# A hybrid decoder step: head 0's new memory as a unit of the projections, its q and k loaded beside the last unit, a reordered input stage, and the ones with the last score

## The chip, the core and the metric

The kernel runs on one NeuronCore of a Trainium2 chip. TensorE (PE) does the matrix products, VectorE (DVE), ScalarE (ACT) and GpSimd (POOL) the element-wise work, and SyncE (SP) issues the transfers between device memory and the core's own memory. Each of these engines takes its instructions in the order in which the program lists them and waits, where it must, for the others by semaphores. The metric is the device time of one execution in microseconds.

## The reference

One inference step of a decoder layer: 528 prompt tokens (16 learned ones and 512) and 8 x 4 sample tokens, 560 columns in all, pass one wide projection; a pooling branch and a matrix memory (mLSTM) of 4 heads with 512 x 512 memories run on it; both are projected, gated, added and normalised.

```python
hn = rmsnorm(x, norm_g)
proj = einsum('btd,dn->btn', hn, w_in)     # a, z, q, k, v, o, z_m, gates i/f, merge gates
# matrix memory, per head:
s   = einsum('bhtd,bhsd->bhts', q, k) * w_intra           # the scores, weighted by decays
num = einsum('bhts,bhsv->bhtv', s, v) + w_inter * einsum('bhtd,bhdv->bhtv', q, C)
kw  = k * w_state
C_new = decay * C + einsum('bhsd,bhsv->bhdv', kw, v)      # the new memory, an output
```

For the prompt the old memory is zero, so that a head's new memory is `kw^T v` over 528 tokens: four row blocks d of 128 rows, each a sum over four full token tiles of 128 and a small one of 16.

## The kernel before

Every product of fp32 numbers is made of three products of split halves (hi and lo): ScalarE rounds a hi copy, VectorE or GpSimd subtracts it for the lo rest. Tokens lie in five tiles (four of 128, a small tile 4 of 48).

**Input stage** (`begin`). The normalised input is transposed tile by tile on TensorE (`turn`); for each tile ScalarE copies hi halves (`hT_hi`) and the whole values (`X`), and VectorE makes `hT_lo`. `project(j, t0, t1, part)` issues products of the first two weight tiles j with columns t0 to t1: part 0 is hi and lo of the input with the weights' hi, part 1 the input's hi with the weights' lo. In parallel SyncE loads the gates' columns into `wg_raw`; they are split into `wg` and multiplied (L576). The sums of `X` (L546) and their halves `Sa`, `Sb`, `Sc`, `Sd` (L553, L551) serve the seven-product scheme of the later projections. `pA`, `pV` and `pT` are engines pinned in program order; what is not pinned is placed by a scheduler.

**Projections** (`projections`). A list of units; each unit has loads, weight splits (`ahead`), products, and evacuations. While unit t multiplies, the splits of unit t+1 and the loads of t+2 are issued, woven into its products. A unit of 256 weight columns (`quad`) has seven products p1 to p7 on TensorE. The last two units are called g6 and g7 here (L167); between them lie memory updates of the sample tokens (`C`, L1131 and L1140).

**Attention** (`attention`). Each head is a set of step lists: `keys` (load k rows, scale by decays: `kw`, L1341), `fetch` and `values` (load v, split into `vr`), `turns` (transpose `kw` on TensorE and split into `kwr`, with 16 rows kept in `st`/`kwst`), `rows` (`prompt_C`: for each d, 12 products `vr`,`kwr` and one `vpt`,`kwst`: the new memory, L1372 and L1373), `decays` (`load_rows` brings `bc`, 960 KB, by a broadcast from `rows_d`; POOL adds the mask, ScalarE takes the exponential, L1325), `parts` (load k and q, split into `khi`, `klo`, `qh`, `ql`), `scores` (L167 again: products of `qh`, `ql` with `khi`, `klo`, 12 for each token tile) and `numerators`. `weave` mixes lists evenly. In the kernel before, head 0's keys and its fetch of v run beside g7, its four turns lie inside and behind g7's products, and its `rows` stand at the start of attention, woven with its decays and parts and with head 1's values and keys.

Rings: the tiles `r` (`RS` = 12 slots) hold loaded k, q, v and `kw`; the ring `hl` holds split weights.

Of the kernel before, what the change touches and what calls it, by code (L numbers as in the profile page):

```python
# [8 lines left out]
F32 = mybir.dt.float32  # L9
# [7 lines left out]
P = 128  # L17
# [83 lines left out]
class Trunk:  # L101
# [264 lines left out]
    def begin(self):  # L366
# [161 lines left out]
        self.split(wg[:, :, 0:64], wg[:, :, 64:128], raw, A, G)  # L528
# [162 lines left out]
    def projections(self, rest):  # L691
# [19 lines left out]
        for h in range(H):  # L711
            if h:
                values += range(len(units), len(units) + 4)
                units += self.unit_v(h)
            units += [self.unit_q(h, 0), self.unit_q(h, 1), self.unit_k(h, 0), self.unit_k(h, 1)]
            n = len(units)
            for j in range(2):
                units += [self.unit_o(h, j), self.unit_zm(h, j)]
            for name, g in fills[h]:
                fill(name, g)  # L720
            if h == 0:
                m = len(units)
            room[h] = n
        end = len(units)
# [12 lines left out]
        self.early = self.head(0)  # L737
# [6 lines left out]
        for t, u in enumerate(units):  # L744
# [13 lines left out]
            ahead = units[t + 1].ahead if t + 1 < end else self.early.keys + self.early.fetch  # L758
# [452 lines left out]
    def attention(self):  # L1211
# [41 lines left out]
    def head(self, h):  # L1253
        nc, O = self.nc, self.O
        V, A, G = nc.vector, nc.scalar, nc.gpsimd
        qT, kT, vr, vc, kwT, og, Pt, own = [], [], [], [], {}, [], [], {}
# [15 lines left out]
        def value(name):  # L1272
            return self.vp.tile([P, 2, HD], F32R, tag="value", name=self.name(name), bufs=17)
# [93 lines left out]
        def prompt_C(d):  # L1367
# [5 lines left out]
            nc.tensor.matmul(pc, kwst[:96], self.vpt[h % 2][:96], start=False, stop=True)  # L1373
# [6 lines left out]
        def score(i):  # L1380
            n, w, t0, o = TILEN[i], SEGW[i], TSTART[i], SEGO[i]
# [114 lines left out]
        u.fetch = each(fetch, 0, 1, 2, 3, 4)  # L1496
        u.turns, u.rows = each(k_rows, 0, 1, 2, 3), each(prompt_C, 0, 1, 2, 3)
# [158 lines left out]
```

## Time and profile before

| what | value |
|---|---|
| median of 3 runs | 1123.2 us (1121.22 to 1124.22) |
| profiled execution, its own time | 1124.12 us |
| its span in the profile | 1122.3 us |
| TensorE busy | 1064.3 us, 95% of the span |
| VectorE busy | 826.9 us, 74% |
| ScalarE busy | 542.1 us, 48% |
| GpSimd busy | 152.5 us, 14% |
| mean granted clock of TensorE | 0.976 of full speed |

The profiled execution lies 0.92 us above the median, and 1.8 us of it lie outside the span. Busy shares are means over all stages; where TensorE sits idle is told by the timeline of the single stages.

### The profile page before, as it was taken

How to read it: one execution, taken by the hardware profiler on the slowest of the kernel's cores; microseconds unless marked ns; L12 is line 12 of the kernel's file. 1: busy time of each engine (PE TensorE's matmuls, PEld its weight loads, DVE VectorE, ACT ScalarE, POOL GpSimd, SP SyncE). 2: the span in 40 equal slices, each digit the busy share in tenths (PEclk: the TensorE clock that was granted, in tenths of full speed). 3: DMA queues.
4: the chain of work that ended last, by engine and by line, in shares of the span. 5: the costliest groups of instructions: out<-in, count | busy, mean ns of one | idle time of the engine just before them, and what ended most of it. 6: DMA issues, size and time to landing. Idle time of an engine off the chain costs nothing.

```text
span 1122.3 us, 19632 instructions
## 1 busy us (share of the span) xinstructions
PE 1064.3 (95%) x7390; PEld 959.8 (86%) x7390; DVE 826.9 (74%) x1342; ACT 542.1 (48%) x1027; POOL 152.5 (14%) x309
## 2 busy tenths in 40 slices
PE   6799999999999999999998999987998789999997
PEld 5689999869999869999778999976887689999876
DVE  5678888787789687889787898855787978444353
ACT  5666545334454445554254554466576665122232
POOL 3100120001200002100001100012454423100000
PEclk9799999999999999999999999988999899999999
DMA  8354556789557688466688387887767889423132
GB/s 201 74 184 124 154 154 216 251 299 279 182 180 259 192 293 265 135 219 229 211 293 252 125 286 256 272 277 246 259 227 242 279 287 353 139 76 95 58 109 85
DMA packets 159615, 233.33 MB, mean 208 GB/s; under 512 B 17321, under 2 KB 82085, under 8 KB 159513
## 3 DMA queue, kind: packets, MB, share of 16 engines
q1 hardware_dynamic: 159521, 232.09, 64.7%
q8 instruction: 58, 0.95, 0.4%
q14 instruction: 36, 0.29, 0.1%
HBM read 160.65 MB, written 70.93 MB: 206 GB/s over the span
## 4 chain that ended last, share of the span: by engine, by line
PE 74%; DMA 12%; DVE 5%; ACT 4%; issue 2%; SPq 2%; POOL 1%; POOLq 0%; DVEq 0%; ACTq 0%
PE ps L167 57%; PE ps L984 7%; PE ps L1131 3%; DMA v_d<-v 2%; PE ps L1372 2%; PE ps L1140 1%; DMA v<-v_d 1%; DMA ra<-in_w_in_dram 1%; PE ps L987 1%; DMA kw<-k_d 1%; PE ps L80 1%; DMA wraw<-in_w_in_dram 1%; DMA x<-in_x_prompt_dram 1%; DMA k<-k_d 1%; PE ps L1415 1%
## 5 line engine op out<-in xcount | busy, mean ns | idle before, releaser
L167 PE MATMUL ps<-hT_hi,w 128*128 128x272 f32 (+1 forms) x752 | 158.7, 292 | 0.0
L167 PEld LDWEIGHTS ps<-hT_hi,w 128*128 128x128 f32 x752 | 123.7, 189 | 4.9 <-issue 3.1
L167 PE MATMUL ps<-hT_lo,w 128*128 128x272 f32 (+1 forms) x376 | 108.7, 289 | 0.0
L1145 DVE SCALAR_TENSOR_TENSOR C<-C,sw,ps 128x512 f32<-128x512 f32 x128 | 89.5, 742 | 10.3 <-PE ps L1140 9.9
L206 DVE TENSOR_TENSOR wb<-rb,wb 128x1024 fp32r<-128x1024 f32 x47 | 57.5, 1223 | 38.9 <-ACT wb L203 38.7
L167 PE MATMUL ps<-hT_hi,wb 128*128 128x272 f32 (+1 forms) x376 | 80.5, 293 | 3.2 <-DVE q L254 3.2
L167 PE MATMUL ps<-Sc_hi,wa 128*128 128x272 f32 (+1 forms) x376 | 79.5, 291 | 3.3 <-ACT u L239 3.2
L167 PE MATMUL ps<-Sb_hi,wb 128*128 128x272 f32 (+1 forms) x376 | 80.0, 292 | 2.0 <-ACT p L239 1.4
L167 PE MATMUL ps<-Sd_hi,w 128*128 128x272 f32 (+1 forms) x376 | 79.8, 292 | 0.0
L203 ACT CAST wa<-ra 128x1024 fp32r<-128x1024 f32 x47 | 49.3, 1050 | 62.3 <-DVE ra L216 52.8
L167 PE MATMUL ps<-Sa_hi,wa 128*128 128x272 f32 (+1 forms) x376 | 78.7, 289 | 0.0
L167 PEld LDWEIGHTS ps<-hT_lo,w 128*128 128x128 f32 x376 | 70.8, 188 | 0.0
L1054 POOL COPY qm<-qw 128x16 f32<-128x16 f32 x32 | 8.1, 286 | 428.4 <-DVE qw L1051 428.4
L167 PEld LDWEIGHTS ps<-hT_hi,wb 128*128 128x128 f32 x376 | 63.1, 191 | 3.6 <-DVE q L254 3.6
L167 PEld LDWEIGHTS ps<-Sc_hi,wa 128*128 128x128 f32 x376 | 62.2, 189 | 4.0 <-ACT u L239 4.0
L167 PEld LDWEIGHTS ps<-Sb_hi,wb 128*128 128x128 f32 x376 | 62.2, 189 | 2.6 <-ACT p L239 1.6
L203 ACT CAST w<-rb 128x1024 fp32r<-128x1024 f32 x47 | 49.4, 1050 | 30.5 <-PE ps L167 17.6
L167 PEld LDWEIGHTS ps<-Sd_hi,w 128*128 128x128 f32 x376 | 62.8, 191 | 0.0
L167 PEld LDWEIGHTS ps<-Sa_hi,wa 128*128 128x128 f32 x376 | 62.0, 188 | 0.0
L206 DVE TENSOR_TENSOR w<-rb,w 128x1024 fp32r<-128x1024 f32 x47 | 57.4, 1222 | 3.2 <-ACT w L203 3.1
L206 DVE TENSOR_TENSOR wa<-ra,wa 128x1024 fp32r<-128x1024 f32 x47 | 57.3, 1219 | 0.0
L203 ACT CAST wb<-rb 128x1024 fp32r<-128x1024 f32 x47 | 49.1, 1046 | 15.9 <-DVE rb L216 15.7
(371 smaller groups left out, 3083.9 us busy)
## 6 DMA issues: line engine op xcount, KB each, us to landing
C<-in_state_C_dram SPq DMA_DIRECT2D x64, 512.0 KB
out_dram<-C SPq DMA_DIRECT2D x64, 512.0 KB
ra<-in_w_in_dram SPq DMA_DIRECT2D x47, 512.0 KB
rb<-in_w_in_dram SPq DMA_DIRECT2D x47, 512.0 KB
wraw<-in_w_in_dram SPq DMA_DIRECT2D x18, 512.0 KB
v<-v_d SPq DMA_DIRECT2D x32, 256.5 KB
wraw<-in_w_branch_mlstm_dram SPq DMA_DIRECT2D x16, 512.0 KB
k_d<-k SPq DMA_DIRECT2D x16, 280.0 KB
```

The costliest lines, as they stand in the source:

```text
L80: return self.tc.keep_in_program_order(getattr(self.engine, op)(*a, **k))
L167: self.nc.tensor.matmul(out, s, m, start=(first and j == 0), stop=(j == len(seq) - 1), skip_group_check=not check)
L203: A.copy(w[name][0], w[s])
L206: V.tensor_tensor(w[name][1], w[s], w[name][0].bitcast(F32), ALU.subtract)
L984: nc.tensor.matmul(pv[i], s, m[:, k2], start=(k == 0 and j == 0), stop=(k == 7 and j == 2))
L987: nc.tensor.matmul(pv[4][:112], self.hS[:, k], m[:, k2], start=(k == 0 and j == 0), stop=(k == 7 and j == 1))
L1054: G.tensor_copy(self.qm[h % 2][:, d, 4 * g:4 * g + 4, 4 * g:4 * g + 4], self.bview(qw)[:, 4 * g:4 * g + 4])
L1131: nc.tensor.matmul(self.pqc[h][r:r + 8], self.qm[h % 2][:, d, b], Cs[bb // 2][:, bb % 2], start=(d == 0 and g == 0), stop=(d == 3 and g == 1),
L1140: nc.tensor.matmul(pu, self.kwst[h, d][r:r + 12, g], self.vst[h][r:r + 12, g], start=True, stop=True, tile_position=(r, 0))
L1145: V.scalar_tensor_tensor(C, C, self.bview(self.sw[h][:, 0])[:, 4 * g + bb, 3:4], pu, ALU.mult, ALU.add)
L1372: nc.tensor.matmul(pc, w[:, s, i], vr[i][:, m], start=(i == 0 and j == 0), stop=False)
L1415: nc.tensor.matmul(pb[:, o:o + mv.shape[-1] - m], s, mv[:, m:], start=(j == 0), stop=(j == last[True]))
```

## The change

Seven edits in four places.

1. Input stage: `parts(2, 3)` and `parts(4)` become `parts(2, 3, 4)`, so that the hi copies of tile 4 stand before the `X` copies of tiles 2 to 4. The last four `project` calls run part 0 of both weight tiles before part 1. The hi copy of `wg` is pinned on ScalarE, in program order behind the `X` copies.
2. A new unit is inserted before g7: it loads v of head 0 (`fetch`) and makes `kw` and `vr` while g6 multiplies, and its products are head 0's four turns and its new memory (`rows`). Its `vr`, `kwr` and `vpt` come from the ring `hl`, its `kwst` from the ring `r`.
3. Beside g7 now run eight loads of head 0's k and q (`ready`); the splits still wait for attention. Head 0's `klo` are all made on VectorE (two of them were POOL's).
4. The small load of constants into `bc` ("ones", `c_sel`) moves from `load_rows` to the last score; attention starts with head 0's decays, woven with its parts and head 1's keys and values.

```diff
         project(1, 0, 256, 1)
-        parts(2, 3)
-        parts(4)
+        parts(2, 3, 4)
         for j in range(2):
             project(j, 256, NT, 0)
+        for j in range(2):
             project(j, 256, NT, 1)
...
         wg = gp.tile([P, NK, P], F32R, name="wg")
-        self.split(wg[:, :, 0:64], wg[:, :, 64:128], raw, A, G)
+        pA.copy(wg[:, :, 0:64], raw)
+        G.tensor_tensor(wg[:, :, 64:128], raw, wg[:, :, 0:64].bitcast(F32), ALU.subtract)
...
+        self.early = e = self.head(0)
+        units.insert(len(units) - 1, Unit(e.fetch, e.keys + e.values, [lambda: [f() for f in e.turns], *e.rows]))
         end = len(units)
...
-        self.early = self.head(0)
...
-            ahead = units[t + 1].ahead if t + 1 < end else self.early.keys + self.early.fetch
+            ahead = units[t + 1].ahead if t + 1 < end else self.early.ready
...
-        u = heads[0]
-        for f in (*u.values[:4], *u.turns, u.values[4]):
-            f()
-        weave(heads[0].rows, heads[0].decays, heads[0].parts, heads[1].values + heads[1].keys)
+        weave(heads[0].decays, heads[0].parts + heads[1].keys + heads[1].values)
...
-            raw = value("vr")
+            raw = self.hl("vr", 2, HD) if early else value("vr")
...
         def part_k(d):
-            t = self.r("k32")
-            nc.sync.dma_start(t, self.k_d[:, 4 * h + d])
-            kT.append(self.parts(t, lambda s: key("k" + s), G if d % 2 else V))
+            if ("k", d) not in qk:
+                fetch_k(d)
+            t = qk.pop(("k", d))
+            kT.append(self.parts(t, lambda s: key("k" + s), G if d % 2 and not early else V))
...
         def score(i):
+            if i == 4:
+
+                nc.sync.dma_start(bc()[48:80, SEGO[4]:SEGO[4] + 48], self.I["c_sel"])
...
         def load_rows():
             nc.sync.dma_start(bc(), self.rows_d[h, :OWI].partition_broadcast(P))
 
-            nc.sync.dma_start(bc()[48:80, SEGO[4]:SEGO[4] + 48], self.I["c_sel"])
-
...
+        u.ready = [f for i in range(4) for f in (*each(fetch_k, i), *each(fetch_q, i))]
```

Where the scheduler puts the instructions shows in their order on the engines, at three places. Line numbers of the changed kernel differ by up to 24 from those of the kernel before.

ScalarE in the input stage, before: `ps_302` and `ps_307` are tile 4, the other `ps` tiles 2 and 3.

```order
L80 COPY X<-ps_249 128x4x128
L138 CAST wg<-wg_raw 128x8x64
L80 COPY X<-ps_254 128x4x128
L80 COPY X<-ps_267 128x4x128
L80 COPY X<-ps_272 128x4x128
L80 CAST hT_hi<-ps_302 128x4x24 x2
L80 CAST hT_hi<-ps_307 128x4x24 x2
L80 COPY X<-ps_302 128x4x24 x2
L80 COPY X<-ps_307 128x4x24 x2
L553 CAST Sa_hi<-X 128x560 x2
```

The same place in the changed kernel:

```order
L80 CAST hT_hi<-ps_302 128x4x24 x2
L80 CAST hT_hi<-ps_307 128x4x24 x2
L80 COPY X<-ps_249 128x4x128
L80 COPY X<-ps_254 128x4x128
L80 COPY X<-ps_267 128x4x128
L80 COPY X<-ps_272 128x4x128
L80 COPY X<-ps_302 128x4x24 x2
L80 COPY X<-ps_307 128x4x24 x2
L80 CAST wg<-wg_raw 128x8x64
L554 CAST Sa_hi<-X 128x560 x2
```

The hi copies of tile 4 moved ahead of all `X` copies, and the copy of `wg`, which stood before three of them, now stands behind all and ahead of `Sa_hi`.

TensorE at the end of the projections, before: the last products of g7 (`hT_hi,wb`), the last turns of head 0 and the first new memory products (L1372).

```order
L167 MATMUL ps_8603<-hT_hi,wb_8586 128x272
L167 MATMUL ps_8603<-hT_lo,wb_8585 128x272
L167 MATMUL ps_8603<-hT_hi,wb_8585 128x272
L1360 MATMUL ps_8854<-ident,st_2_747 96x128
L1359 MATMUL ps_8865<-ident,kw_8686 128x128 x4
L1360 MATMUL ps_8866<-ident,st_3_749 96x128
L1372 MATMUL ps_8897<-vr_8817,kwr_8836 128x512 x3
L1372 MATMUL ps_8897<-vr_8820,kwr_8836 128x512 x3
L1372 MATMUL ps_8897<-vr_8823,kwr_8836 128x512 x3
```

The changed kernel, first where the turns now stand: in front of `hT_hi,wb`, which are here the last products of g6.

```order
L1378 MATMUL ps_8643<-ident,kw_8503 128x128 x4
L1379 MATMUL ps_8644<-ident,st_0_743 96x128
L1378 MATMUL ps_8655<-ident,kw_8525 128x128 x4
L1379 MATMUL ps_8656<-ident,st_1_745 96x128
L1378 MATMUL ps_8667<-ident,kw_8550 128x128 x4
L1379 MATMUL ps_8668<-ident,st_2_747 96x128
L1378 MATMUL ps_8679<-ident,kw_8556 128x128 x4
L1379 MATMUL ps_8680<-ident,st_3_749 96x128
L167 MATMUL ps_8473<-hT_hi,wb_8448 128x272
L167 MATMUL ps_8473<-hT_lo,wb_8447 128x272
```

and the end of the new unit, where g7 (`w_1406`) begins:

```order
L1394 MATMUL ps_8795<-vr_8576,kwr_8686 128x512 x3
L1394 MATMUL ps_8795<-vr_8594,kwr_8686 128x512 x3
L1394 MATMUL ps_8795<-vr_8597,kwr_8686 128x512 x3
L1394 MATMUL ps_8795<-vr_8616,kwr_8686 128x512 x3
L1395 MATMUL ps_8795<-vpt_8635,kwp_8689 128x512
L167 MATMUL ps_8813<-hT_hi,w_1406_8704 128x272
L167 MATMUL ps_8813<-hT_lo,w_1406_8704 128x272
```

All four turns now lie in one piece ahead of g6's last product, and all four new memory blocks ahead of g7, so that scores follow g7 directly.

ScalarE at the start of attention, before (`bc_8894` is head 0's decay rows, L1325 the exponentials; `vr_8885` belongs to head 1):

```order
L138 CAST vr_8885<-v_1425_8883 128x512
L138 CAST khi_8890<-k_1427_8888 128x560
L1325 ACT_TABLE_LOAD
L1325 ACTIVATE bc_8894<-bc_8894,acol 128x512
L1325 ACTIVATE bc_8894<-bc_8894,acol 128x400
L1325 ACTIVATE bc_8894<-bc_8894,acol 128x272
L1325 ACTIVATE bc_8894<-bc_8894,acol 128x144
L1325 ACTIVATE bc_8894<-bc_8894,acol 48x48
```

and in the changed kernel:

```order
L138 CAST khi_8992<-k_1437_8883 128x560
L138 CAST qh_8996<-q_1438_8885 128x544
L138 CAST khi_9000<-k_1439_8900 128x560
L1332 ACT_TABLE_LOAD
L1332 ACTIVATE bc_8976<-bc_8976,acol 128x512
L138 CAST qh_9006<-q_1441_8924 128x544
L1332 ACTIVATE bc_8976<-bc_8976,acol 128x400
L1332 ACTIVATE bc_8976<-bc_8976,acol 128x272
L1332 ACTIVATE bc_8976<-bc_8976,acol 128x144
L1332 ACTIVATE bc_8976<-bc_8976,acol 48x48
```

Before, one `khi` stood ahead of the exponentials and the other key and query halves behind; now all but the last `qh` stand ahead, and this last one behind the table load and the first exponential.

## Rows read from the trace of the kernel before

**Rows 1.** Timeline of TensorE, input stage (start us, duration us, instruction, [idle before <-releaser]).

```profile
35.22 0.62 PE L80 MATMUL ps<-hT_hi,whi 128*128 128x304 f32 x1 [8.99 <-ACT hT_hi L80]
41.32 0.30 PE L80 MATMUL ps<-hT_hi,whi 128*128 128x304 f32 x1
44.79 0.37 PE L576 MATMUL ps<-hT_lo,wg 128*128 128x280 f32 x1
49.92 0.40 PE L984 MATMUL ps<-wlo,hT_hi 128*128 128x512 f32 x1
```

**Rows 2.** Timeline of ScalarE, input stage.

```profile
32.80 0.62 ACT L138 CAST wg<-wg_raw 128x512 fp32r<-128x512 f32 x1 [7.06 <-DMA wg_raw<-in_w_in_dram]
34.76 0.69 ACT L80 CAST hT_hi<-ps 128x96 fp32r<-128x96 f32 x4
37.21 1.31 ACT L553 CAST Sa_hi<-X 128x560 fp32r<-128x560 f32 x2 [0.85 <-DVE X L546]
```

**Rows 3.** Timeline of VectorE, input stage and first gates.

```profile
35.20 0.75 DVE L80 TENSOR_TENSOR hT_lo<-ps,hT_hi 128x96 fp32r<-128x96 f32 x4 [8.28 <-ACT hT_hi L80]
39.05 0.73 DVE L551 TENSOR_TENSOR Sa_lo<-X,Sa_hi 128x560 fp32r<-128x560 f32 x1
47.95 0.50 DVE L582 SCALAR_TENSOR_TENSOR ig<-ps,gbi,ig 4x280 f32<-4x280 f32 x1 [1.16 <-ACT zf L581]
```

**Rows 4.** Timeline of GpSimd, input stage.

```profile
33.50 1.26 POOL L141 TENSOR_TENSOR wg<-wg_raw,wg 128x512 fp32r<-128x512 f32 x1 [9.95 <-ACT wg L138]
```

**Rows 5.** Timeline of TensorE, its two waits between 76 and 100 us.

```profile
79.56 0.40 PE L167 MATMUL ps<-Sb_hi,wb 128*128 128x272 f32 x1 [1.41 <-ACT p L239]
92.12 0.39 PE L167 MATMUL ps<-Sb_hi,wb 128*128 128x272 f32 x1 [0.62 <-DVE wb L206]
```

**Rows 6.** By stretch: length; PE, PEld, DVE, ACT, POOL busy; granted clock; DMA share; GB/s.

```profile
72.00:80.00 8.00, 6.59 (x41) 5.79 (x40) 3.60 (x4) 7.97 (x19) 0.00 (x0) 1.00 0.54 152
100.00:690.00 590.00, 583.33 (x4237) 524.18 (x4236) 481.90 (x773) 282.15 (x501) 42.62 (x138) 0.99 0.70 223
743.00:775.00 32.00, 20.81 (x74) 15.06 (x74) 13.76 (x23) 21.74 (x47) 8.00 (x21) 0.78 0.85 289
749.00:762.00 13.00, 13.00 (x47) 10.46 (x48) 3.36 (x6) 8.00 (x18) 3.83 (x10) 0.80 0.73 269
770.00:785.00 15.00, 13.09 (x78) 11.36 (x78) 11.25 (x24) 9.30 (x25) 4.19 (x8) 0.73 0.83 284
```

**Rows 7.** Timeline of TensorE, end of projections and start of attention.

```profile
728.14 0.29 PE L167 MATMUL ps<-hT_hi,w 128*128 128x272 f32 x1
748.87 12.56 PE L1372 MATMUL ps<-vr,kwr 128*128 128x512 f32 x43 [3.44 <-DVE kwr L141]
769.72 0.76 PE L167 MATMUL ps<-qh,klo 128*128 128x512 f32 x1 [4.08 <-ACT qh L138]
```

**Rows 8.** SyncE's queue, issues of head 0's kw and bc loads.

```profile
734.64 2.00 SPq L1339 DMA_DIRECT2D kw<-k_d  x2
746.39 0.32 SPq L1488 DMA_DIRECT2D bc<-rows_d  x1
```

**Rows 9.** Timeline of VectorE, the third kw of head 0.

```profile
739.19 0.71 DVE L1341 SCALAR_TENSOR_TENSOR kw<-kw,wsb 128x528 f32<-128x528 f32 x1 [3.35 <-DMA kw<-k_d]
```

**Rows 10.** Timeline of ScalarE, first decays of head 0.

```profile
752.60 1.28 ACT L1325 ACT_TABLE_LOAD   x1 [1.51 <-DMA bc<-rows_d]
753.89 2.19 ACT L1325 ACTIVATE bc<-bc,acol 128x512 f32<-128x512 f32 x5
```

**Rows 11.** Groups of ScalarE by shape, 690 to 800 us (busy us, mean ns | idle before).

```profile
L138 ACT CAST khi<-k 128x560 fp32r<-128x560 f32 x7 | 4.6, 658 | 0.8 <-DMA k<-k_d 0.8
```

**Rows 12.** Groups of VectorE by shape, 743 to 800 us.

```profile
L141 DVE TENSOR_TENSOR ql<-q,qh 128x544 fp32r<-128x544 f32 x6 | 4.3, 720 | 1.7 <-ACT qh L138 1.7
```

**Rows 13.** Timeline of GpSimd, first and last step of head 0's D chain.

```profile
783.94 0.66 POOL L1426 COPY D<-bc 128x112 f32<-128x112 f32 x1 [0.61 <-DVE bc L1385]
793.88 0.28 POOL L1430 TENSOR_TENSOR D<-D,bc 48x48 f32<-48x48 f32 x1
```

More of the change, by code (lines that the diff above doesn't have):

```diff
@@ L1255, in head @@
         V, A, G = nc.vector, nc.scalar, nc.gpsimd
-        qT, kT, vr, vc, kwT, og, Pt, own = [], [], [], [], {}, [], [], {}
+        qT, kT, vr, vc, kwT, og, Pt, own = [], [], {}, [], {}, [], [], {}
+        early = h == 0
         def bc():
@@ L1287, in load_v @@
             t = v32.pop(i) if i in v32 else rows_in(i)
-            raw = value("vr")
+            raw = self.hl("vr", 2, HD) if early else value("vr")
             self.split(raw[:m, 0], raw[:m, 1], t[:m, :HD], A, V)
-            vr.append(raw)
+            vr[i] = raw
             if i == 4:
+                if early:
+                    own["vpt"] = self.hl("vpt", HD)
+                    for k in range(4):
+                        G.tensor_copy(own["vpt"][:, k * P:(k + 1) * P], self.zeros)
+                else:
+                    own["vpt"] = self.vpt[h % 2]
                 for j, p in enumerate((0, 1, 0)):
-                    nc.sync.dma_start(self.vpt[h % 2][32 * j:32 * j + 16].bitcast(F32), raw[:16, p].bitcast(F32))
+                    nc.sync.dma_start(own["vpt"][32 * j:32 * j + 16].bitcast(F32), raw[:16, p].bitcast(F32))
         def centre(i):
@@ L1325, in decays, with fetch_q, fetch_k @@
             A.activation(w, w, AF.Exp, bias=self.acol[:n, i, h:h + 1])
+        qk = {}
+        def fetch_q(d):
+            t = qk["q", d] = self.r("q32")[:, :NO]
+            nc.sync.dma_start(t, self.q_d[:, 4 * h + d])
+        def fetch_k(d):
+            t = qk["k", d] = self.r("k32")
+            nc.sync.dma_start(t, self.k_d[:, 4 * h + d])
         def load_q(d):
-            t = self.r("q32")[:, :NO]
-            nc.sync.dma_start(t, self.q_d[:, 4 * h + d])
+            if ("q", d) not in qk:
+                fetch_q(d)
+            t = qk.pop(("q", d))
             qh, ql = key("qh"), key("ql")
@@ L1360, in k_rows @@
             nc.tensor.transpose(ps2[:96, :P], self.st2[d].bitcast(F32), self.ident)
-            w = value("kwr").rearrange("p s (i d) -> p s i d", i=4)
+            w = (self.hl("kwr", 2, HD) if early else value("kwr")).rearrange("p s (i d) -> p s i d", i=4)
             self.split(w[:, 0], w[:, 1], ps.rearrange("p (i d) -> p i d", i=4), A, V)
-            kwst = self.hp.tile([P, P], F32R, tag="kwst", name=self.name("kwst"), bufs=3)
+            if early:
+                kwst = self.r("kwp", F32R)[:, :P]
+            else:
+                kwst = self.hp.tile([P, P], F32R, tag="kwst", name=self.name("kwst"), bufs=3)
             A.copy(kwst[:96], ps2[:96, :P])
@@ L1372, in prompt_C @@
                     nc.tensor.matmul(pc, w[:, s, i], vr[i][:, m], start=(i == 0 and j == 0), stop=False)
-            nc.tensor.matmul(pc, kwst[:96], self.vpt[h % 2][:96], start=False, stop=True)
+            nc.tensor.matmul(pc, kwst[:96], own["vpt"][:96], start=False, stop=True)
             c32 = self.r("c32")[:, :HD]
```

## The prediction, made before the changed kernel ran

> **What bounds the kernel now.** I began with the busy time by stretch [rows 6]. From 100 to 690 us TensorE is busy 583.3 of 590 us at a clock of 0.99: there every microsecond by which its work starts earlier is kept, and nothing else counts. So a gain can come only from stretches in which TensorE stands idle or runs at half clock, and the change touches two. The first is the input stage: TensorE waits 8.99 us for a hi copy, until 35.22 [rows 1], and its next matmuls take 0.62 us each, against 0.30 at 41.32 [rows 1]: that is the lower level of its clock, 1.2 GHz, against 2.4. The second is the passage to attention: between 743 and 775 us it is busy 20.81 of 32 us, idle 11.2 [rows 6], and the granted clock is 0.80 between 749 and 762 and 0.73 between 770 and 785 [rows 6]. In time this costs 13 x 0.20 + 15 x 0.27 = 6.7 us. Both places together hold some 27 us; the question is how much of them another engine takes back.
>
> **Input stage, step by step.** ScalarE shows why TensorE waits: the copy of `wg` stands among the `X` copies and waits 7.06 us for its load, until 32.80, and tile 4's hi copies (0.69 us) stand behind it at 34.76 [rows 2]. VectorE has been free since 35.20 - 8.28 = 26.9 us [rows 3]. With the hi copies first, they lie in front of the wait; tile 4 was transposed before TensorE's idle time began at 35.22 - 8.99 = 26.2 us [rows 1]. So `hT_lo` is there by 26.9 + 0.75 = 27.7 us [rows 3], TensorE waits about 1 us, and if its clock stays up, the 48 products take twice the 3.4 us that the second 24 took between 41.32 and 44.79 [rows 1]: done at about 34.5.
>
> The gates come next. They need `wg`, whose load does not move: it lands at 32.80, its copy takes 0.62, its lo half on POOL 1.26 us from 33.50 [rows 2, 4], so that the gates can start at about 35, against 44.79 [rows 1]: 9.8 us earlier on TensorE. This isn't the gain. `Sa_hi` stands behind `wg` on ScalarE and can't start before 33.4; its first half takes 0.65, so VectorE starts `Sa_lo` at 34.1 instead of 39.05 [rows 2, 3]. Its chain from there to the lo half of the next weights ran without a gap to 47.95 - 1.16 = 46.8 [rows 3], 7.7 us, so it now ends at 41.8. The first product with those weights, at 49.92 [rows 1], comes at 41.9: 8.0 us earlier. The gate arithmetic behind it on VectorE, at 47.95 after 1.16 us of waiting for ScalarE [rows 3], starts at 41.9: 6.1 earlier. This chain leads over ScalarE, which is busy 7.97 of 8 us between 72 and 80 us [rows 6], to the wait of 1.41 us at 79.56 [rows 5]. There TensorE, 8.0 ahead, meets a ScalarE that is 6.1 ahead, and gives the difference back. The wait of 0.62 at 92.12 [rows 5] is for work that is then ahead and mostly goes. The term is **-6.6 us**, with bounds of -5.0 (only `Sa_lo`'s shift, 39.05 - 34.1, passes on) and -8.0 (all of TensorE's). Which part of `project` comes first costs nothing: the same 48 products, all operands present. POOL's two `hS` casts change places with `wg`'s lo half; they are covered by TensorE's products up to 34.5.
>
> **Passage to attention.** The new unit moves work and adds none: four turns, 52 products. That the new memory left its place behind g7 takes away the wait of 3.44 us ahead of it [rows 7], and the rest of the 11.2 us idle is no longer where it was, so the sum is that idle time against the new waits, counted from the changed order.
>
> - Turns in one piece, ahead of g6's last product: they need `kw`, and the products after them `kwr`. VectorE's added work there, some 13 splits and scalings of about 0.7 us [rows 9, 12], lies beside g6 and a new unit of about 12 us. I take 0.4 us; bounds 0 and the 3.44 of [rows 7].
> - First score behind g7: ScalarE must evacuate g7, then make `khi` and `qh` (0.66 each [rows 11]), VectorE `klo` (0.72 [rows 12]). Before, this was hidden by the new memory's products. About 2.0 us, bounds 1.4 and 4.08, the longest such wait now [rows 7].
> - Within the first score each d needs `klo` and `ql`, 1.4 us of VectorE [rows 12], for 0.7 us of TensorE: three times 0.7, 2.1 us; this includes `klo` moved from POOL to VectorE. The last `qh` stands behind the first exponential, which waits for `bc`. Its load took 752.60 - 746.39 = 6.2 us [rows 8, 10]; issued as g7 ends, it would leave some 4 us more. `bc`'s issue stands right behind `qc`'s, which ends during g7's last products, so I take none of it, and keep 4.4 as the bound.
> - Head 1's turns and its first new memory block: 1.0 us for `kw` and `kwr`, bounds 0 and 3.4.
> - Its second block: `kwr` stands on ScalarE behind the conversion of head 0's D and behind head 1's five exponentials (2.19 us [rows 10]). D comes from POOL, whose chain took 783.94 to 794.16, 10.2 us [rows 13]. From the first score on: 0.7 + 10.2 + 0.7 + 2.2 + three conversions of 0.7 = 15.9; TensorE's scores and turns meanwhile, 13.09 x 0.73 = 9.6 us at full clock [rows 6] less 1.4 for those of the first score, and 12 of the 43 products that took 12.56 at 0.80, 2.8 us [rows 6, 7], make 11. That is 4.9 us at most; as the chain had 1.5 us of waits for ScalarE and VectorE, I take 3.2.
>
> New waits: 0.4 + 2.0 + 2.1 + 1.0 + 3.2 = 8.7 us for 11.2, **-2.5 us**. The half clock I leave as it is: the new memory of head 0 escapes it (2.6 us), but waits of 2 to 3 us have been followed by it in this trace (3.44, then 0.80 [rows 6, 7]), and head 1's memory now stands behind such a wait. Bounds: 0 if waits take everything, -6.7 more if no half clock is left. The moved load of ones (`c_sel`) only takes an issue out of SyncE's way; it is covered by the scores. The k and q loads beside g7 are under products, at a DMA share of 0.85 now [rows 6].
>
> On ScalarE the table load takes 1.28 us and the exponential starts 0.01 us behind it [rows 10]. The Trainium skill (ScalarE: Activation LUTs, What ACT_TABLE_LOAD costs) puts a drain of about 1.38 us to each load, 2.66 in all. By the row the last `qh` waits for 1.28 us, by that rule for 1.38 us more, if it can't hide in the wait for `bc` that stands before the load here (1.51 us [rows 10]); the sum would then be -7.7 instead of -9.1.
>
> **Sum.** -6.6 - 2.5 = -9.1: the profiled execution of 1124.1 us (its span 1122.3, 1.8 around it) becomes 1115.0. It lies 0.9 above the median of the runs, so the median is about 1114.
>
> **Rivals.**
> Only the start counts: the waits in front of the scores take all 11.2 us. For it speaks that TensorE has no other work there any more; against, that all k and q lie loaded. -6.6, 1116.6 as a median.
> Full gain: scores follow g7 at full clock. For it: every operand is loaded; against: VectorE needs twice TensorE's time per score. -8.0 at the start, -6 of the idle time, -5 of the half clock: 1104.
> The start is eaten: if gates or weights in the first 100 us hang on a load instead of VectorE's chain, all comes back by 100 us, as `wg`'s load does not move. Then -2.5, perhaps -3: 1120.5.
> Slower: all four turns stand ahead of everything, so one late `kw` holds up TensorE. The third and fourth are issued behind stores of g6's results on SyncE, now at 734.64 [rows 8], and the first of them was scaled at 739.19 [rows 9], 4.55 us later. The turns would now start at 728.1 [rows 7], the third at 729; with 0.9 for scaling, the issue must come by 723.6. If it stays at 734.6, TensorE waits 11.0 us, and 2.6 of half clock follow: -9.1 + 13.6 = +4.5, a median of 1127.7. It makes the kernel slower by over 3.4 us from an issue at about 733.5 on. Against it: in the changed order `kw` needs no result later than g6's.
>
> **Chances.** Forecast (1110.5 to 1116.5) 0.57, start only (to 1118.5) 0.17, full gain (1103 to 1110) 0.12, start eaten 0.08, slower 0.06. A difference of 0.3%, 3.4 us, is about what can be told from none: faster means below 1119.8, slower above 1126.6. Faster takes the first three and a fifth of the fourth: 0.87; same 0.07; slower 0.06. The range leaves out the ends: 1106.5 to 1119.
>
> **What would show it.** Right: TensorE's first 304-column product near 27 us at 0.30 us each, the gates at 35, the product of 49.92 at 42, a longer wait near 72 us; in the passage no wait over 4 us, several of 1 to 3 ahead of scores and of head 1's memory. Wrong: half clock from 27 to 40 again; a wait over 3 us inside the turns; g7 waiting for its weights; a first score later than 3 us behind g7.

## The result, and the profile after

| | before | after |
|---|---|---|
| median of the runs compared, us | 1123.71 (4 runs, 1121.22 to 1126.98) | 1113.36 (4 runs, 1112.18 to 1113.63) |
| profiled execution / its span, us | 1124.1 / 1122.3 | 1112.18 / 1110.4 |
| mean granted clock | 0.976 | 0.987 |

The ratio is 0.9907, with a 95% interval of 0.9889 to 0.9926: the change takes 8.3 to 12.5 us off, 10.4 by the medians. About 1114 was predicted.

Timeline of TensorE in the input stage, which answers to [rows 1], and its two waits after 70 us, which answer to [rows 5]:

```profile
27.93 0.37 PE L80 MATMUL ps<-hT_hi,whi 128*128 128x304 f32 x1
29.15 0.41 PE L80 MATMUL ps<-hT_lo,whi 128*128 128x304 f32 x1 [0.85 <-DVE hT_lo L80]
29.39 0.30 PE L80 MATMUL ps<-hT_hi,whi 128*128 128x304 f32 x1
...
35.96 0.37 PE L577 MATMUL ps<-hT_lo,wg 128*128 128x280 f32 x1
...
41.51 0.50 PE L986 MATMUL ps<-wlo,hT_hi 128*128 128x512 f32 x1 [0.25 <-DVE wlo L975]
...
72.73 0.39 PE L167 MATMUL ps<-Sb_hi,wb 128*128 128x272 f32 x1 [2.90 <-ACT p L239]
76.31 0.39 PE L167 MATMUL ps<-Sc_hi,wa 128*128 128x272 f32 x1 [0.32 <-ACT u L239]
```

The wait of 8.99 us is a wait of 0.85, and the products behind it take 0.30 us, the time of the upper clock level (granted clock 1.00 from 28 to 34 us), from the third on. What lies ahead of the edits came late in this execution: tile 4's first transpose stands at 25.95 us, in before at 24.10, so that against [rows 1] the gain of the first products looks 1.9 us too small. Where the lead is handed back shows too: the wait for ScalarE's `p` is 2.90 us where [rows 5] had 1.41. In after the clock stayed at 1.00 behind it, but in eight of the twelve profiles with the new start it fell to the lower level there for 3 to 7 us (e1: 0.57 from 72 to 76 us), a price that the prediction doesn't have.

ScalarE, GpSimd and VectorE in the same stage, which answer to [rows 2 to 4]:

```profile
31.37 0.62 ACT L80 CAST wg<-wg_raw 128x512 fp32r<-128x512 f32 x1 [1.41 <-DMA wg_raw<-in_w_in_dram]
31.89 1.22 ACT L554 CAST Sa_hi<-X 128x560 fp32r<-128x560 f32 x2
```

```profile
32.07 1.78 POOL L529 TENSOR_TENSOR wg<-wg_raw,wg 128x512 fp32r<-128x512 f32 x1 [2.11 <-ACT wg L80]
```

```profile
29.99 2.70 DVE L547 TENSOR_TENSOR X<-X 128x560 f32<-128x560 f32 x4 [0.56 <-ACT X L80]
32.60 1.84 DVE L552 TENSOR_TENSOR Sa_lo<-X,Sa_hi 128x560 fp32r<-128x560 f32 x1
...
40.23 1.23 DVE L975 TENSOR_TENSOR wlo<-wraw,whi 128x1024 fp32r<-128x1024 f32 x1
41.36 0.49 DVE L583 SCALAR_TENSOR_TENSOR ig<-ps,gbi,ig 4x280 f32<-4x280 f32 x1
```

All eight `X` copies now lie ahead of `wg`, so ScalarE's wait fell from 7.06 to 1.41 us and VectorE could sum `X` from 29.99 on. The load itself was there 1.4 us earlier, which isn't the edits' doing (see e2). `Sa_lo` takes 1.84 us, not 0.73, while GpSimd works on `wg`.

The passage by stretch, which answers to [rows 6] (length; PE, PEld, DVE, ACT, POOL busy; granted clock; DMA share; GB/s):

```profile
690.00:719.70 29.70, 29.70 (x237) 27.21 (x236) 26.09 (x48) 15.26 (x34) 2.13 (x4) 1.00 1.00 350
719.70:738.00 18.30, 18.12 (x103) 14.44 (x102) 12.45 (x17) 9.11 (x18) 0.00 (x0) 1.00 0.42 151
738.00:754.00 16.00, 13.79 (x89) 12.10 (x88) 6.22 (x10) 10.29 (x23) 4.69 (x10) 0.90 0.77 244
754.00:775.00 21.00, 14.58 (x86) 11.82 (x85) 15.41 (x30) 15.13 (x40) 14.77 (x27) 0.91 0.84 295
775.00:797.00 22.00, 21.85 (x130) 19.70 (x131) 16.24 (x37) 15.75 (x39) 3.44 (x3) 0.93 0.88 289
```

and, overlapping these, the 32 us that [rows 6] shows from 743 on, and 13 us from the first score on:

```profile
743.00:775.00 32.00, 23.36 (x134) 18.91 (x132) 21.19 (x38) 23.96 (x58) 19.46 (x36) 0.89 0.82 276
750.00:763.00 13.00, 10.56 (x37) 7.55 (x38) 10.63 (x23) 9.57 (x25) 7.65 (x13) 0.74 1.03 353
```

From the first turn (719.7) to 797 us TensorE is idle 0.18 + 2.21 + 6.42 + 0.15 = 9.0 us; [rows 6] had 11.2, and 8.7 was predicted. Over the 32 us from 743 the clock is 0.89 where it was 0.78; half clock is left behind the first score's wait (0.74 from 750 to 763) and behind the one at 775.15. This last stretch lies just outside of the 32 us; from 715 to 800 us the clock is 0.94, in before 0.90.

Timeline of TensorE there, which answers to [rows 7]:

```profile
721.70 0.66 PE L1378 MATMUL ps<-ident,kw 128*128 128x128 f32 x4 [0.18 <-ACT kwp L1386]
...
725.30 3.04 PE L1394 MATMUL ps<-vr,kwr 128*128 128x512 f32 x12
...
750.14 0.47 PE L167 MATMUL ps<-qh,klo 128*128 128x512 f32 x1 [2.05 <-DVE klo L141]
750.77 0.80 PE L167 MATMUL ps<-ql,khi 128*128 128x512 f32 x1 [0.17 <-DVE ql L141]
...
756.01 0.49 PE L167 MATMUL ps<-qh,klo 128*128 128x512 f32 x1 [1.48 <-ACT qh L138]
756.77 0.50 PE L167 MATMUL ps<-ql,khi 128*128 128x512 f32 x1 [0.27 <-DVE ql L141]
...
768.38 3.00 PE L1394 MATMUL ps<-vr,kwr 128*128 128x512 f32 x12 [1.14 <-DVE kwr L141]
772.97 0.47 PE L1395 MATMUL ps<-vpt,kwst 96*128 96x512 f32 x1 [1.59 <-POOL vs L1317]
775.15 4.33 PE L1394 MATMUL ps<-vr,kwr 128*128 128x512 f32 x12 [1.71 <-DVE kwr L141]
```

The turns and head 0's new memory run without a wait for `kwr`; behind g7 come several waits of 1 to 2 us, ahead of scores and of head 1's memory.

To see where time is won or lost I took each instruction of TensorE and VectorE that both profiles hold, and its lead over the profile of before. These are median leads, in us, at six places (us of before's span), and what the passage gave (785-800 less 690-720):

```
                          100    300   690-720  785-800   840-860   end     passage
after                     7.1    9.8     8.4     11.2      14.7     11.9      2.8
e12, after once more      6.8    5.3     5.5      7.5       9.8      9.1      2.0
e3_hi_late                6.9    8.5     8.0      9.7      10.8     11.3      1.7
e4_wg_free                3.3    4.3     5.1      7.7       8.9      6.5      2.6
e11_wg_dve                6.4    8.5     7.4      9.6      12.9     11.7      2.2
e1_start_only             6.4    7.5     7.8      6.3       6.0      6.8     -1.5
e2_unit_only              2.5    2.0     0.3      2.1       3.4      2.8      1.8
e5_load_late              6.8    7.4     5.0      3.3       4.5      2.2     -1.7
e6_klo_pool               6.7    5.6     5.5      7.7       7.1      3.9      2.2
e7_ones_early             5.6    7.0     1.9      2.6       4.6      4.5      0.7
e8_d_major                4.6    6.2     3.6      7.3       7.6      6.0      3.7
e9_decays_mid             6.9    9.5     9.2     16.6      14.1     19.4      7.4
e10_d_decays              6.6    5.5     5.9     10.9      11.7     12.8      5.0
```

Two cautions. Between 100 and 690 us, where the code is that of before, the lead of one and the same kernel went from 7.1 to 8.4 in one profile and from 6.8 to 5.5 in another. And e1, whose passage is that of before, lost 1.5 there. Over all thirteen profiles the lead changes between 100 and 690 us by -3.7 to +2.3, by -0.2 on average, so on average it is kept, as the prediction took it. A single profile's lead is good to a few us over the middle, to about 1.5 over the passage; the timed ratios decide.

### The profile page after: what moved, and what is told of

Its sections match the earlier page's. It is cut to its first block, busy times and chain, and to the rows that moved or that the text cites. A ratio compares the mean times of both kernels' runs of the same rounds, so it can differ in the third digit from the quotient of the medians.

```text
span 1110.4 us, 19654 instructions
## 1 busy us (share of the span) xinstructions
PE 1057.9 (95%) x7390; PEld 953.1 (86%) x7390; DVE 832.2 (75%) x1344; ACT 543.4 (49%) x1027; POOL 158.2 (14%) x311
## 4 chain that ended last, share of the span: by engine, by line
PE 72%; DMA 10%; DVE 10%; ACT 4%; issue 2%; SPq 1%; POOL 0%; DVEq 0%; POOLq 0%; ACTq 0%
PE ps L167 60%; PE ps L986 2%; PE ps L1394 2%; PE ps L1133 2%; DMA v_d<-v 2%; DMA out_dram<-C 2%; PE ps L1142 1%; DMA bc<-rows_d 1%; DMA x<-in_x_sample_dram 1%; PE ps L1440 1%; DVE C L1147 1%; DMA vs_d<-vsp 1%; DMA rb<-in_w_in_dram 1%; DVE wlo L975 1%; DVE vr L141 1%
```

## The experiments

Kernels that ran together share the runs of before: 1124.12 us (15 runs) for e1 to e4, 1126.44 (17) for e5 to e8, 1123.86 (11) for e9 to e12. Ratios are against these.

**e1 and e2: the two places apart.** e1 is before with the input stage's edits alone, e2 the rest of the change with the input stage of before.

```diff
 e1, on before:
-        parts(2, 3)
-        parts(4)
+        parts(2, 3, 4)
...
-        self.split(wg[:, :, 0:64], wg[:, :, 64:128], raw, A, G)
+        pA.copy(wg[:, :, 0:64], raw)
+        G.tensor_tensor(wg[:, :, 64:128], raw, wg[:, :, 0:64].bitcast(F32), ALU.subtract)
```

> The kernel before with the input stage's three edits alone (hi copies of tile 4 first, part 0 of both weight tiles first, wg's hi copy pinned behind the X copies). By the prediction's first term it is 6.6 us faster than the kernel before (bounds 5.0 and 8.0), and TensorE's work is about 7 us earlier at 100 us and stays so to 690 us. By the rival that the start is eaten by a load, 0 to 2 us. In the trace of the changed kernel the work stood 7.1 us earlier at 100 us.

Measured: 1118.41 us, ratio 0.9954 (0.9924 to 0.9983), -5.2 us.

> The kernel before with all edits but those of the input stage. By the prediction's second term 2.5 us faster than the kernel before (bounds 0 and 9). By the rival that the new waits take everything 0; by the rival of full gain about 11. In the trace of the changed kernel the numerators of head 0 had gained 2.8 us more than the input stage gave, and the end 3.5, so 2.5 to 3.5 is what the theory now says.

Measured: 1119.78 us, 0.9965 (0.995 to 0.998), -3.9 us. Each place alone makes the kernel faster, and the two add up to 9.1 us, against 10.4 for both (by their intervals 1.9 to 8.5 and 2.2 to 5.6). The rival by which only the start counts falls. e2 leads by 2.5 us at 100 us with an input stage that is that of before. ScalarE in e2 shows why:

```profile
30.73 0.62 ACT L138 CAST wg<-wg_raw 128x512 fp32r<-128x512 f32 x1 [4.55 <-DMA wg_raw<-in_w_in_dram]
```

The load of `wg_raw` was there 2.07 us earlier than in [rows 2], and `Sa_lo` followed at 36.99 instead of 39.05. So the profile of before is late by chance: SyncE issued this load at 28.38 us in it, and between 26.21 and 27.71 in the thirteen others. Some 1 to 2 us of every lead at 100 us in the table come from there; by time the start is worth 5.2 rather than the 6.4 of e1's lead.

**e3 and e4: which edit of the start counts.** e3 puts tile 4's hi copies back behind the `X` copies and keeps `wg`'s copy in program order; e4 does the reverse, with `wg`'s copy free for the scheduler, as it was.

```diff
 e3, on after:
-        parts(2, 3, 4)
+        parts(2, 3)
+        parts(4)
 e4, on after:
-        pA.copy(wg[:, :, 0:64], raw)
-        G.tensor_tensor(wg[:, :, 64:128], raw, wg[:, :, 0:64].bitcast(F32), ALU.subtract)
+        self.split(wg[:, :, 0:64], wg[:, :, 64:128], raw, A, G)
```

> The changed kernel with the hi copies of tile 4 behind the X copies of tiles 2 and 3 again; wg stays pinned behind all. Theory: what counts is when Sa_hi frees VectorE's chain, and that hangs on wg alone, so TensorE starts its 304-column products some 2 us later than in the changed kernel, the gates 1 to 2 us later, but VectorE's gate chain starts at the same time within 0.5 us: 9.5 to 10.4 us faster than the kernel before. Rival: TensorE's wait for the hi copies is what counts, and then it loses 2 us or more against the changed kernel: 8 us or less.

Measured: 1113.38 us, 0.9906 (0.9883 to 0.9928), which is the time of after. TensorE's first 304-column product in e3, which stands 3.77 us behind tile 4's first transpose, in after 1.98:

```profile
28.45 0.41 PE L80 MATMUL ps<-hT_hi,whi 128*128 128x304 f32 x1 [1.63 <-ACT hT_hi L80]
```

> The changed kernel with wg's split unpinned; ScalarE's order then has wg's copy behind the first X copy again, with the hi copies of tile 4 ahead of it. Theory: the X copies wait for wg's load, VectorE's sums and Sa_lo come as late as before (within 1 us), and the gate chain gives TensorE's lead back by 100 us: of the start 0.5 to 1.5 us are left, 3 to 4.5 us faster than the kernel before in all. Rival: the hi copies alone carry the gain of the start: 9 us or more faster.

Measured: 1118.54 us, 0.9954 (0.9934 to 0.9975). ScalarE and VectorE in e4:

```profile
30.61 0.62 ACT L138 CAST wg<-wg_raw 128x512 fp32r<-128x512 f32 x1 [4.53 <-DMA wg_raw<-in_w_in_dram]
31.13 2.12 ACT L80 COPY X<-ps 128x512 f32<-128x512 f32 x7
```

```profile
33.28 2.70 DVE L546 TENSOR_TENSOR X<-X 128x560 f32<-128x560 f32 x4 [5.63 <-ACT X L80]
35.90 0.73 DVE L551 TENSOR_TENSOR Sa_lo<-X,Sa_hi 128x560 fp32r<-128x560 f32 x1
```

In e4 the first 304-column product starts at 26.15 us, 1.95 behind tile 4's first transpose, which is as early as in after, and yet e4 loses 5 us against it: `wg`'s copy, behind the first `X` copy, holds seven of them back, VectorE waits 5.63 us, `Sa_lo` starts at 35.90 instead of 32.60, and TensorE's lead of 6.8 us at 60 us is down to 3.3 at 100. So it is the place of `wg`'s copy that carries the start, and putting the hi copies first, which saves TensorE 1.8 us of waiting, is worth nothing that these runs can tell. The third edit of the stage, part 0 of both weight tiles before part 1, stands in both kernels and was not tried alone.

**e5: k and q loaded after the last unit.** The loads beside the last unit are taken out; each is issued where its split stands.

```diff
-            ahead = units[t + 1].ahead if t + 1 < end else self.early.ready
+            ahead = units[t + 1].ahead if t + 1 < end else []
```

> The changed kernel, but head 0's k and q are loaded in attention, behind bc's load, instead of beside g7. Theory: nothing on TensorE covers these loads any more (first k about 5 us after its issue, and bc's 960 KB ahead of it), so the first score comes 4 to 7 us later than the 2.05 us behind g7 that the changed kernel shows: 4 to 6 us slower than the changed kernel, that is 4 to 6 us faster than the kernel before. Rival: the first score waits for VectorE's and ScalarE's splits anyway, and the loads cost under 1.5 us.

Measured: 1121.92 us, 0.9964 (0.9942 to 0.9985), 6.4 us slower than after's ratio gives. The two longest waits of TensorE from 715 to 800 us by group (sum, times, longest):

```profile
PE ps L1394 <- DVE kwr L141: 6.0, 1, 6.0
PE ps L167 <- ACT qh L138: 5.9, 1, 5.9
```

The early loads are a condition of the passage's gain: without them it is a loss (-1.7 in the table).

**e6 and e7: the two small edits.** e6 puts every second `klo` of head 0 back on GpSimd, e7 the load of the ones back into the load of `bc`.

```diff
 e6, on after:
-            kT.append(self.parts(t, lambda s: key("k" + s), G if d % 2 and not early else V))
+            kT.append(self.parts(t, lambda s: key("k" + s), G if d % 2 else V))
 e7, on after (and its issue in score(4) taken out):
             nc.sync.dma_start(bc(), self.rows_d[h, :OWI].partition_broadcast(P))
+            nc.sync.dma_start(bc()[48:80, SEGO[4]:SEGO[4] + 48], self.I["c_sel"])
```

> The changed kernel with the odd klo of head 0 on GpSimd again. Theory: GpSimd takes 1.4 us for one against 0.7, and in the changed kernel it is busy with zero copies until 752.3 us and with masks from 753.4 us, so the first score's second part comes 1 to 2 us later; but the last part waits for qh anyway, so 0 to 2 us slower than the changed kernel. Rival: VectorE's chain of eight splits is what the score waits for, and two of them less make it 1 us faster.

Measured: 1119.77 us, 0.9932 (0.9907 to 0.9957). TensorE waits 2.6 us for GpSimd's `klo` and 5.4 for `kwr` (2.9 in after), yet the passage gives 2.2 us, between the 2.0 and 2.8 of the two profiles of after.

> The changed kernel with the small load of ones back in load_rows. Theory: SyncE stands at it until bc's load has landed, as in the kernel before (up to 4.1 us), and the loads of head 1's kw and v behind it come 3 to 5 us later; head 1's turns among the scores and its first new memory block wait for them: 2 to 5 us slower than the changed kernel. Rival: they are loaded early enough, no difference above 1 us (the prediction put this edit at nothing).

Measured: 1119.8 us, 0.9933 (0.9908 to 0.9957). The stall that the theory of e7 needs isn't in its trace: the loads of head 1's v are issued 7.2 us behind `bc`'s, in after 6.7, so 0.5 us later and not 3 to 5; and 3.7 us of its lead go between 100 and 690 us, in code that it doesn't touch. Both kernels lie 2.8 us above after by ratio, with intervals that overlap its own; what these edits are worth stays open, somewhere from nothing to 6 us.

**e8: scores by d.** Head 0's scores run over d outside and tiles inside, in five banks, so that TensorE has five products for each `klo` and `ql`; the turns of head 1 come behind them.

```diff
-            weave(u.scores, n.turns, u.centre, n.decays)
+            if h == 0:
+                for f in u.by_d:
+                    f()
+                weave(n.turns, u.centre, n.decays)
+            else:
+                weave(u.scores, n.turns, u.centre, n.decays)
```

> The changed kernel with head 0's scores in another order: the products of one d for all five token tiles, then the next d, with five PSUM banks open; head 1's turns follow. Theory: the first score waits because VectorE needs 1.4 us per d and TensorE 0.7; with 1.7 us of products per d this wait goes, the evacuations follow in one piece, and GpSimd's D chain ends earlier: the sum of TensorE's waits from 748 to 776 us falls from about 8 to 5 us or less, and the kernel is 2 to 4 us faster than the changed one. Rival: all that follows (v and kw of head 1) is bound by loads and VectorE, and the time moves to the wait ahead of head 1's new memory: within 1 us.

Measured: 1116.35 us, 0.9901 (0.9872 to 0.993). TensorE's waits behind the scores:

```profile
768.67 0.66 PE L1383 MATMUL ps<-ident,kw 128*128 128x128 f32 x4 [1.12 <-DVE bc L1430]
774.52 5.04 PE L1399 MATMUL ps<-vr,kwr 128*128 128x512 f32 x12 [5.08 <-DVE kwr L141]
```

The waits within the first score are gone, and one of 5.08 us stands ahead of head 1's memory; from 748 to 776 us all waits together are 8.4 us, not the 5 or less of the theory. So taking VectorE's pace per score out of the way doesn't shorten the passage. In this order head 1's turns come behind all scores, which by itself makes `kwr` late.

**e9 and e10: head 1's exponentials later.** In after, head 1's decays are woven with head 0's scores, and their five exponentials stand on ScalarE ahead of head 1's second `kwr`. e9 weaves them with head 1's rows instead; e10 does that on top of e8.

```diff
 e9, on after:
-            weave(u.scores, n.turns, u.centre, n.decays)
+            weave(u.scores, n.turns, u.centre, n.decays if h else [])
...
-                weave(n.rows if h + 2 < H else n.rows[:-2], u.sums, n.parts, last)
+                weave(n.rows if h + 2 < H else n.rows[:-2], u.sums, n.parts, last, [] if h else n.decays)
```

> The changed kernel with head 1's decays (bc load, masks, exponentials) among head 1's new memory instead of among head 0's scores. ScalarE then has the second kwr of head 1 ahead of the conversion of D and of the five exponentials. Theory (the prediction's last new wait): that wait, 1.71 us in the changed kernel, falls below 0.5 us, and TensorE's waits from 748 to 790 us fall by 1 to 2 us; 0.5 to 2 us faster than the changed kernel, too little for the runs to tell. Rival: the decays come later and head 1's scores or numerators wait for them: no gain, or up to 2 us slower.

Measured: 1110.98 us (1104.73 to 1113.29), 0.9869 (0.9844 to 0.9894). ScalarE in after, then in e9:

```profile
769.81 0.65 ACT L138 CAST dh<-D 128x544 fp32r<-128x544 f32 x1 [1.02 <-POOL D L1455]
770.37 2.18 ACT L1332 ACTIVATE bc<-bc,acol 128x512 f32<-128x512 f32 x5
...
773.06 0.56 ACT L138 CAST kwr<-ps 128x512 fp32r<-128x512 f32 x1
```

```profile
768.80 0.57 ACT L138 CAST kwr<-ps 128x512 fp32r<-128x512 f32 x1
...
769.40 0.65 ACT L138 CAST dh<-D 128x544 fp32r<-128x544 f32 x1
...
771.65 2.02 ACT L1332 ACTIVATE bc<-bc,acol 128x512 f32<-128x512 f32 x4
```

The same stretch of 20 us by engine, after and then e9:

```profile
760.00:780.00 20.00, 15.56 (x89) 13.38 (x89) 16.26 (x26) 14.84 (x34) 11.50 (x21) 0.89 0.74 243
```

```profile
760.00:780.00 20.00, 18.52 (x110) 15.62 (x109) 15.70 (x23) 14.52 (x33) 11.37 (x19) 1.00 0.70 227
```

The second `kwr` is cast 4.3 us earlier, its wait of 1.71 us is 0.23, the 1.59 ahead of it is gone, and the clock stays up: 3.0 us more of busy TensorE, at 1.00 instead of 0.89. The passage gives 7.4 us instead of 2.8. The edit also changed TensorE's order: the scheduler put the first two products with `vpt` behind the third block, and the wait of 1.59 us stood ahead of the first of them. So e9 shows that the 1.71 us come from ScalarE's order, and not how the rest of its gain divides.

> Scores of head 0 by d as in the run before, and head 1's decays later as well. There the first block of head 1's new memory waited 5.08 us for kwr on VectorE. Theory: both orders together leave 2 us ahead of the first score and 2 to 4 us ahead of head 1's memory: 2 to 4 us faster than the changed kernel. Rival: the loads of head 1's v set the time of its first block, and the sum of waits from 748 to 790 us stays at 8 to 9 us: within 1 us of the changed kernel.

Measured: 1109.93 us (1108.89 to 1111.27), 0.9873 (0.9857 to 0.9889). One `kwr` wait of 4.5 us is left; on top of e9, the order of e8 adds nothing that these runs can tell.

**e11: the lo half of `wg` on VectorE.**

```diff
-        G.tensor_tensor(wg[:, :, 64:128], raw, wg[:, :, 0:64].bitcast(F32), ALU.subtract)
+        V.tensor_tensor(wg[:, :, 64:128], raw, wg[:, :, 0:64].bitcast(F32), ALU.subtract)
```

> The changed kernel with wg's lo half on VectorE instead of GpSimd. In the changed kernel the first Sa_lo took 1.84 us instead of 0.73 while GpSimd made wg's lo half, which took 1.78 instead of 1.26. Theory: the two engines get in each other's way in memory; alone, Sa_lo takes 0.73 and wg's lo half about 0.7 us on VectorE, so that VectorE's chain to the gates ends 0 to 0.8 us earlier, and the kernel is the same within 1 us. Rival: Sa_lo is slow for another reason (what it reads was just written) and stays at 1.4 us or more; then the chain ends 0.7 us later.

Measured: 1113.13 us, 0.9909 (0.989 to 0.9927): no gain. VectorE in e11:

```profile
31.88 0.69 DVE L529 TENSOR_TENSOR wg<-wg_raw,wg 128x512 fp32r<-128x512 f32 x1 [1.81 <-ACT wg L80]
...
33.79 1.39 DVE L552 TENSOR_TENSOR Sa_lo<-X,Sa_hi 128x560 fp32r<-128x560 f32 x2
...
41.45 0.49 DVE L583 SCALAR_TENSOR_TENSOR ig<-ps,gbi,ig 4x280 f32<-4x280 f32 x1
```

`Sa_lo` is back to 0.70 us for one, but the 0.69 us is now VectorE's own and it waits 1.81 us for `wg`; `ig` starts at 41.45, against 41.36 in after.

**e12: after once more**, for its scatter beside e9 to e11.

> The changed kernel unedited, beside the others on one chip. By its first runs 10.4 us faster than the kernel before (8.3 to 12.5). For the trace: TensorE 7 to 8.5 us ahead at 60 us, 6 to 7.2 at 100 us; between 100 and 690 us the lead can change by 2 to 3 us either way though the code there is the same, if stretches at half clock there (one at 283, one at 594 in the kernel before, one at 587 in the changed one) come and go from run to run.

Measured: 1114.52 us (1109.56 to 1116.87), 0.9906 (0.9885 to 0.9927): the ratio repeats to 0.0001. TensorE leads by 8.9 us at 60 us, a little more than expected, by 6.8 at 100 and by 5.5 at 690 to 720. e9 lies 0.37% below it (4.2 us, where 0.5 to 2 was expected) and e10 0.33%; their intervals overlap its own a little, so each is better than after by the passage's profile and likely, not surely, by time.

## Why the prediction was right, step by step

**The start (-6.6).** Right in size: TensorE and VectorE lead by 8.3 us at 60 us and, past the waits at 72.73 and 76.31, by 7.1 at 100; leads at 100 us are 6.4 to 7.1 in after, e1, e3, e11 and e12. By time the start is -5.2 us in e1, and -6.5 as what after has over e2. The product of [rows 1] predicted at 41.9 came at 41.51, `ig` at 41.36 for 41.9, the gates at 35.96 for 35, the longer wait at 72.73. One reading of [rows 1] was loose: 0.62 us is the time of the first two products behind the wait, the others at the lower level took 0.46 (granted clock 0.50 from 28 to 41 us).

Two steps inside were off and cancelled, which is luck. I had written that `wg`'s load "does not move" from 32.80: it was there at 31.37 in after, 31.73 in e3, 30.61 in e4 and, without any edit of this stage, 30.73 in e2, so `Sa_lo` started at 32.60 instead of 34.1. And I had carried over VectorE's chain from `Sa_lo` on at its old length, 7.7 us: it took 8.9, from 32.60 to the end of `wlo` at 41.46. The 1.1 us more is `Sa_lo` at 1.84 us for 0.73. GpSimd's subtraction, issued at 32.07 while VectorE's last sum ran until 32.69, takes 0.52 us more than its 1.26 us of [rows 4]; `Sa_lo`, begun at 32.60, ends at 34.44, 0.60 us behind GpSimd's end at 33.84. In e12 VectorE had no sum running when GpSimd began (GpSimd, then VectorE):

```profile
31.93 1.29 POOL L529 TENSOR_TENSOR wg<-wg_raw,wg 128x512 fp32r<-128x512 f32 x1 [3.11 <-ACT wg L80]
32.45 1.37 DVE L552 TENSOR_TENSOR Sa_lo<-X,Sa_hi 128x560 fp32r<-128x560 f32 x1 [0.90 <-ACT Sa_hi L554]
```

Ten profiles have this pair. In seven no sum was running: GpSimd took 1.29 to 1.31 us and `Sa_lo` 1.37 to 1.39. In after, e1 and e6 one was, and they took 1.49 to 1.78 and 1.57 to 1.84. In all ten `Sa_lo` ends 0.60 us behind GpSimd: the one that comes second waits for the other's instruction to finish, and e11, where GpSimd has no part, shows 0.70. So some 0.65 us of the 1.1 come with the order, and the rest with a sum that was late in this execution. The Trainium skill (SBUF — State Buffer, Who interferes with whom) says that VectorE and GpSimd share a port pair under an exclusive lock, that a VectorE instruction with two SBUF inputs contends for it with a GpSimd instruction that reads SBUF, and that the order of issue decides who blocks; this case's traces agree, with these numbers. I hadn't weighed that edit: in before the two didn't meet [rows 3, 4].

**Which edit brings the start.** My text started from "with the hi copies first", and made `wg`'s place a follower. e3 and e4 show it the other way round. My own sum said so too, since it went by `Sa_lo`'s start and not by TensorE's, but the gain of TensorE's first 9 us was never the term.

**The passage (-2.5).** Right in size: 2.8 and 2.0 us in two profiles of after, 1.7 to 2.6 in e2, e3, e4 and e11, and -3.9 us by e2's time. Term by term, predicted and measured in after: turns 0.4, 0.18; first score 2.0, 2.05; within it 2.1, and 0.17 + 1.48 + 0.27 = 1.9; head 1's turns and first block 1.0, and 0.39 + 1.14 + 1.59 = 3.1; second block 3.2 (4.9 less 1.5 would have been 3.4), and 1.71. So the last two terms were off by 2.1 and 1.5 in opposite directions, and that the sum came to 9.0 for 8.7 is luck there. The split within the first score was wrong: most of it is the last `qh`, behind the wait for `bc` of which I had taken "none". `bc` was issued at 747.44 and waited for until 753.41. VectorE's pace, which I had blamed, cost 0.4. The 1.59 us, which no term of mine had, stand ahead of the last product of the first block, which reads `vpt`. The profile names GpSimd's `vs` for them in after and the load of `vpt` in e12 (2.29 us). It is the load: in six of the seven profiles with this wait the product starts 2.4 to 2.7 us behind the last issue of `vpt` (after, e2, e3, e4, e11, e12; 3.6 in e7), and in e9, where it stands 8.7 us behind that issue, it waits for nothing. The reason given for the second block, `kwr` behind D's conversion and the five exponentials on ScalarE, is what e9 took away, and with it went these 1.71 us but for 0.23.

**The table load.** ScalarE in after:

```profile
753.41 1.28 ACT L1332 ACT_TABLE_LOAD   x1 [1.02 <-DMA bc<-rows_d]
754.70 0.72 ACT L1332 ACTIVATE bc<-bc,acol 128x512 f32<-128x512 f32 x1
755.33 0.63 ACT L138 CAST qh<-q 128x544 fp32r<-128x544 f32 x1
```

and GpSimd, which waits for the same load:

```profile
753.41 2.25 POOL L1331 TENSOR_TENSOR bc<-bc,mask 128x112 f32<-128x112 f32 x4 [1.15 <-DMA bc<-rows_d]
```

Both engines start as `bc` lands, at 753.41, and the exponential follows the table load by 0.01 us. A load that no wait stands ahead of, later in the same profile:

```profile
847.32 0.77 ACT L138 CAST Ph<-bc 128x272 fp32r<-128x272 f32 x3
848.10 1.28 ACT L1332 ACT_TABLE_LOAD   x1
849.40 0.72 ACT L1332 ACTIVATE bc<-bc,acol 128x512 f32<-128x512 f32 x1
```

It starts as the cast ahead of it ends, and the exponential follows by 0.02 us. The Trainium skill (ScalarE: Activation LUTs, What ACT_TABLE_LOAD costs) puts a further drain of about 1.38 us to each load. The trace doesn't agree: no such time shows at either place, with a wait or without, so the load costs its 1.28 us here, and the sum with the drain (-7.7) would have been further from the result.

**The half clock**, left as it was, turned out a little better (0.94 for 0.90 from 715 to 800 us), for which the sum has nothing. I had also given no gain to the heads behind the passage, where after won 3.5 us more by 850 us and e12 2.3; why is not shown. The end of the two profiles, 11.9 and 9.1 us ahead, lies on both sides of the 10.4 measured; that 10.4 is more than 9.1 is within what the runs can tell apart.

**The rivals.** Only the start: ruled out by e2. Full gain: needed the waits gone and the clock up; e8 removed its stated obstacle and gained no time that can be told from after, e9 came nearest. Start eaten: didn't happen, and e4 shows what it would have taken. Slower: the third and fourth `kw` were in time; the turns' only wait was 0.18 us.

## What to carry to other kernels

Where one engine casts for several others, find which of its casts the longest chain behind it needs, and keep a cast that waits for a load out of that chain's way; the engine that visibly waits may be ahead by more than it can keep. When work moves away from a gap, the sum of the new waits against the old idle time, each from a row, gave the idle time of the gap to 0.3 us (9.0 for 8.7), but two of its five terms were off by 1.5 and 2.1: such a sum is to be trusted to a few us. A wait can cost half clock on top: behind the 1.71 us at 775.15 the twelve products of head 1's memory took 4.33 us instead of 2.91 to 3.04, so the order on the engine that feeds them can be worth more than its waits show (e9 gave 4.6 us more than after in the passage, 3.1 of it by these waits).

## What the chip showed unexpectedly

VectorE and GpSimd delayed one another by 1.1 and 0.5 us in one pair of instructions (above), and the profile shows the delay as busy time of the instruction that waits. From 690 to 719.7 us the DMA engines were busy at a share of 1.00, 350 GB/s, and TensorE lost nothing: 29.70 of 29.70 us. The same small load (`wg_raw`) was waited for until 30.61, 31.37, 31.73 and 32.80 us in e4, after, e3 and before, which issue it at the same place of the program; the scatter is already there when SyncE gets to it, at 26.21, 26.72, 27.43 and 28.38 us, 4.3 to 4.7 us earlier. And waits with half clock behind them come and go in code that isn't touched: before waits 2.43 us ahead of the product at 282.10 and shows 0.57 from 283 to 287 us, where after waits 0.81 us ahead of the same product and stays at 1.00; e7 waits 2.83 us at 424.98 and shows 0.57 from 426 to 430, where after waits 1.73 us and stays at 1.00. Others are in both: after shows 0.59 from 587 to 591, behind a wait of 2.51 us, and before 0.59 from 594 to 598, behind one of 2.88 us at the same product. Such places are where the leads of after and e7 change between 100 and 690 us.
